# A two-layer decoder trunk: the first loads in smaller pieces, six warm-up matmuls instead of nine, and the last output tile in three column pieces

## The chip, the cores and the metric

The kernel runs on one core of one Trainium2 chip. The metric is the device time of a whole execution, in microseconds (us); lower is better. A core has five engines with an instruction stream each: TensorE (PE; its loads of the stationary operand are listed as PEld), VectorE (DVE), ScalarE (ACT), GpSimd (POOL) and SyncE (SP), which here only issues transfers (DMAs). They wait for each other by semaphores. The compiler of the kernel lays out the order of the instructions on each engine, and that order is kept when the program runs.

## What is computed

The reference is a trunk of two layers over 512 tokens with 16 learned "meta" tokens in front, 528 in all, with a width of 1024, in 32-bit floats. Cut to what matters:

```python
for l in range(DEPTH):                      # 2 layers
    h = rmsnorm(h_res, norm_gain[l])
    proj = h @ w_in[l]                      # 1024 -> 4640 columns
    u_pool, z_pool, c_q, c_kv, k_rope, z_mla, g_pool, g_mla = split(proj)
    y_pool = (pool_mix(u_pool, ...) * silu(z_pool)) @ pool_w_up[l]
    o_mla  = mla(c_q, c_kv, k_rope, pos, ...)           # 8 heads, causal attention
    y_mla  = (o_mla * silu(z_mla)) @ mla_w_up[l]
    merged = sigmoid(g_pool) * y_pool + sigmoid(g_mla) * y_mla
    h_res  = h_res + merged @ w_out[l]      # 1024 -> 1024
return h_res[:, N_META:]                    # the 512 tokens
```

## The kernel before

Activations are kept transposed: 128 features on the partitions, tokens along the columns. A width of 1024 is thus eight "depth" pieces of 128. To keep the precision of 32-bit numbers on PE, each operand is split into a high part (a rounded copy, made by ACT) and a low part (what the rounding left, made by DVE), and each product is three matmuls: high x high, high x low, low x high. This is `mm3` (lines 203 to 207): line 204 multiplies the high weights with the high tokens, 205 the high weights with the low tokens, 206 the low weights with the high tokens. Each of them loads its own 128x128 stationary tile of weights.

All large products go through one list, `plan`. Each entry (`Gemm`) is one tile of 128 output features; `stream()` (line 213) walks the list. It fetches the weights in chunks of up to 512 columns (four depth pieces, 256 KB), four chunks ahead, splits them in `wload` (lines 191 to 201), and multiplies. The tokens of a tile are cut into `segs`, column pieces with a PSUM buffer each: for every chunk of weights all pieces are walked, and within a piece four depth pieces, three matmuls each. When the last depth piece of a column piece is done, its evacuation `evac` runs. In layer 0 the pieces are two of 264 tokens (`FULL`, line 126), in layer 1 one of 512 (`XTOK`), since the meta tokens are dropped. The attention of eight heads, the statistics for the norms and the splits run beside this stream.

The start is written by hand, lines 141 to 173. The first chunk of weights (the first half of tile `ckv0`) is fetched into the buffer `rinv` by ACT's queue; SP issues the gains `gn` (24 KB), the first token tile `xb[:, 0]` (264 KB), the first chunk of `ckv1` into `raw`, and the second token tile. The other six token tiles, two more chunks and two tables are issued by `other_loads` (line 164); each waits until the transfer named `first` has landed, which is that of the gains:

```python
act.dma_start(early[0][:, 0:512], win[0, MT_CKV, :, 0:512])
first = sp.dma_start(gn, gains)
sp.dma_start(xb[:, 0, :T], xT[:, 0, :])
```

Line 157 then gives PE nine matmuls of 128 columns on a tile of ones, whose result nobody reads. A token tile is scaled with its gain and split by `split_h` (line 362): line 366 on ACT writes the high part `hh`, line 368 on DVE the low part `hl`; for the first tile this is done in two halves of 264 tokens, for the others at once. The split of the weights is line 199 (ACT) and 200 (DVE); the results of the first two chunks are in buffers named `th`, later ones in `whi` and `wlo`. The products of `ckv0` go to PSUM buffers named `S`, those of `ckv1` to `mm`.

The end is the product with `w_out` in layer 1, tiles `o0` to `o7`. Their evacuation is `ev_o`: SP fetches the residual rows from the scratch `scr` into a buffer `tmp` (line 1055; there are three such buffers), DVE adds them to half the product (line 1061), SP writes the output `yT` (line 1065). `o7` is the last work of the program, and the only tile of layer 1 that is cut into two column pieces, of 256 tokens each.

Of the kernel before, what the change touches and what calls it, by code (L numbers as in the profile page):

```python
# [9 lines left out]
F32 = mybir.dt.float32  # L10
# [3 lines left out]
AF = mybir.ActivationFunctionType  # L14
# [4 lines left out]
P = 128  # L19
DEPTH = 2  # L20
D = 1024
SEQ = 512
NM = 16
T = SEQ + NM
HALF = T // 2
# [10 lines left out]
MT_CKV = 0  # L36
# [21 lines left out]
BACK = 7800.0  # L58
LATE = 13000.0
RET = 12500.0  # L60
WARM = 9
NB = 10


# [16 lines left out]
def trunk(ctx, tc, xT, xrow, mrow, pos, win, wkr, wqb, wkb, wvb, wgr, wpu, wmu, wout, gains, const, yT):  # L81
    nc = tc.nc
    pe, act, dve, gp, sp = nc.tensor, nc.scalar, nc.vector, nc.gpsimd, nc.sync
# [11 lines left out]
    def nm(s):  # L95
        uid[0] += 1
        return f"{s}_{uid[0]}"

    def slot(tag, dt=F32, bufs=1, w=W):
        return sl.tile([P, w], dt, tag=tag, name=nm(tag), bufs=bufs)  # L100
# [7 lines left out]
    def wide():  # L108
        return tp.tile([P, NB * P], F32R, tag="th", name=nm("th"), bufs=2)
# [20 lines left out]
    gn = cp.tile([P, DEPTH * N_GAIN], F32, name="gn")  # L130
    xb = cp.tile([P, 8, W], F32, name="xb")
    early = []

    def fetch(src, n, raw, eng):
        eng.dma_start(raw[:, :n], src)
        return raw

    def rawt():
        return wp.tile([P, 512], F32, tag="raw", name=nm("raw"), bufs=3)

    early.append(slot("rinv"))
    act.dma_start(early[0][:, 0:512], win[0, MT_CKV, :, 0:512])
    first = sp.dma_start(gn, gains)
    sp.dma_start(xb[:, 0, :T], xT[:, 0, :])
    early.append(fetch(win[0, MT_CKV + 1, :, 0:512], 512, rawt(), sp))
    sp.dma_start(xb[:, 1, :T], xT[:, 1, :])
    xt = [xb[:, k] for k in range(8)]
# [7 lines left out]
    wps = pp.tile([P, 512], F32, tag="o", name="wps", bufs=1)  # L155
    for i in range(WARM):
        pe.matmul(wps[:, 0:P], ones, ones, start=True, stop=True)  # L157
# [31 lines left out]
    loads = [0]  # L189

    def wload(src, n, spare):
        raw = early.pop(0) if early else fetch(src, n, rawt(), sp)
        loads[0] += 1
        if loads[0] <= 2 or spare:
            t = wide()
            hi, lo = t[:, 0:512], t[:, 512:1024]
        else:
            hi, lo = (wp.tile([P, 512], F32R, tag=t, name=nm(t), bufs=3) for t in ("whi", "wlo"))
        act.activation(hi[:, :n], raw[:, :n], AF.Copy)  # L199
        dve.tensor_sub(lo[:, :n], raw[:, :n], hi[:, :n].bitcast(F32))  # L200
        return hi, lo

    def mm3(out, wh, wl, xh, xl, start, stop):
# [9 lines left out]
    def stream():  # L213
# [5 lines left out]
        def load(i):  # L219
            g_, c = flat[i]  # L220
            n = min(512, g_.width - c)
            return wload(g_.src[:, c:c + n], n, g_.spare)
# [120 lines left out]
    class Layer:  # L343
# [728 lines left out]
        def register(self, nxt):  # L1072
            l, XS = self.l, self.XS
            wi = lambda t: win[l, t]
            hs, ys, cs = (lambda: self.hs), (lambda: self.ys), (lambda: self.cs)

            def add(name, src, width, **kw):
                plan.append(Gemm((l, name), src, width, **kw))

            for m in range(2):  # L1080
                if (l, m) == (0, 1):
                    plan[-1].alloc = sct
                add(f"ckv{m}", wi(MT_CKV + m), D, evac=self.ev_ckv(m), xs=hs, segs=FULL)
            def cq(m):
                add(f"cq{m}", wi(MT_CQ + m), D, evac=self.ev_cq(m), xs=hs, segs=XS)

            def kk(p):
                add(f"k{p}", wkb[l, p], 256, evac=self.ev_k(p), xs=cs, segs=FULL)

            for m in range(5):  # L1090
                cq(m)
            for m in range(4):
                add(f"u{m}", wi(MT_U + m), D, evac=self.ev_u(m), xs=hs, segs=FULL)
                kk(m)
            def zp(m):
                add(f"zp{m}", wi(MT_ZP + m), D, evac=self.ev_silu(self.zps, "xa", m), xs=hs, segs=XS)

            def y(m):
                add(f"y{m}", wgr[l, m], P, evac=self.ev_y(m), xs=lambda: [self.ys[m]], segs=XS)

            add("v", wvb[l], 1024, body=self.v_body)
            zp(0)
            zp(1)
            y(0)
            zp(2)
            y(1)
            zp(3)
            y(2)
            cq(5)
            y(3)  # L1110
            for r in range(2):
                add(f"qr{r}", wqb[l, r], 768, evac=self.ev_qr(r), xs=lambda: self.cqs, segs=XS)
            for p in range(4):
                add(f"qn{p}", wqb[l, 2 + p], 768, evac=self.ev_qn(p), xs=lambda: self.cqs, segs=XS)
            for m in range(8):
                add(f"pu{m}", wpu[l, m], 512, evac=self.ev_pu(m), xs=ys, segs=XS)
            for m in range(4):
                add(f"zm{m}", wi(MT_ZM + m), D, evac=self.ev_silu(self.zms, "u", m), xs=hs, segs=XS)
            for m in range(8):
                add(f"gp{m}", wi(MT_GP + m), D, evac=self.ev_gp(m), xs=hs, segs=XS)  # L1120
            for m in range(8):
                add(f"gm{m}", wi(MT_GM + m), D, evac=self.ev_gm(m), xs=hs, segs=XS)
            for m in range(8):
                add(f"mu{m}", wmu[l, m], 512, evac=self.ev_mu(m), xs=lambda: self.ogs, segs=XS)
                plan[-1].spare = m % 2 == 1
                if (l, m) in ((0, 2), (0, 5)):
                    plan[-1].alloc = sct
            mg = lambda: self.mg
            for m in range(8):
                add(f"o{m}", wout[l, m], D, evac=self.ev_o(m, nxt), xs=mg,  # L1130
                    segs=[(NM, NM + SEQ // 2), (NM + SEQ // 2, T)] if self.last and m == 7 else XS)
                if (l, m) == (0, 1):
                    plan[-1].alloc = sct

# [151 lines left out]
```

## Time and profile before

| what | us |
|---|---|
| median of 3 runs | 758.31 |
| lowest and highest | 758.05, 759.73 |
| the profiled execution, whole | 758.87 |
| its span, first to last instruction | 756.0 |
| PE busy | 750.0 (99%) |
| DVE busy | 549.7 (73%) |
| ACT busy | 395.8 (52%) |

The profile is of one execution; its times are counted from the start of the span. A row of the timeline gives the start and the duration in us, the engine, the line of the kernel, the operation, what is written and read, shapes (partitions x elements), a count if several equal instructions were merged, and in brackets how long the engine had been idle and what ended it. Matmuls are pipelined: the duration of one is longer than the distance to the next, so their pace is read from the starts. SPq and ACTq are the engines' queues on which transfers are issued; the duration there is that of the issue, and the data land later. In a row of groups, after the count stand the busy time in us and the mean of one in ns. PEclk is the clock that was granted to PE, in tenths.

### The profile page before, as it was taken

The page shows a single profiled execution, that of the slowest core. Times are in us where ns is not written, and L with a number is a line of the kernel's source. Part 1 is how long each engine was busy: PE and PEld are TensorE (multiplying, and loading weights), DVE is VectorE, ACT ScalarE, POOL GpSimd, SP SyncE. Part 2 cuts the span into 40 slices and gives each one's busy share as a digit, 9 for nine tenths or more (in the row PEclk, how much of TensorE's full clock was granted, in tenths as well). Part 3 has the DMA queues.
Part 4 walks back from the last instruction along what each step waited for, and adds up shares of the span by engine and source line. Part 5 has one row for each costly group of instructions (what it writes and reads, how often), then busy time and mean ns, then how long its engine had stood idle before and what let it go on. Part 6 is the DMA issues. An engine that isn't in the chain of part 4 may idle for free.

```text
span 756.0 us, 14327 instructions
## 1 busy us (share of the span) xinstructions
PE 750.0 (99%) x5030; PEld 683.9 (90%) x5030; DVE 549.7 (73%) x1211; ACT 395.8 (52%) x864; POOL 219.0 (29%) x267
## 2 busy tenths in 40 slices
PE   9999999999999999999999999999999999999998
PEld 9999999999999999999997898887788888878887
DVE  5587787358999978784376487774578999966942
ACT  6755656545566656443364355455445656653321
POOL 2026305104463520160220263032054535101400
PEclk9999999999999999999999999999999999999999
DMA  8533223343756558425643333234438666773472
GB/s 287 173 101 101 85 86 87 119 120 120 212 166 192 167 152 216 116 86 166 182 124 98 102 94 90 82 90 125 127 110 230 171 159 202 191 178 89 130 229 83
DMA packets 72852, 106.57 MB, mean 141 GB/s; under 512 B 14102, under 2 KB 34966, under 8 KB 72780
## 3 DMA queue, kind: packets, MB, share of 16 engines
q1 hardware_dynamic: 72636, 105.39, 48.1%
q8 instruction: 39, 0.64, 0.4%
q14 instruction: 33, 0.27, 0.1%
q10 hardware_dynamic: 144, 0.26, 0.1%
HBM read 89.76 MB, written 15.86 MB: 140 GB/s over the span
## 4 chain that ended last, share of the span: by engine, by line
PE 95%; DMA 2%; DVE 2%; issue 0%; SPq 0%; ACT 0%; ACTq 0%
PE mm L206 28%; PE mm L204 28%; PE mm L205 28%; PE S L204 2%; PE S L205 2%; PE S L206 2%; DMA attE<-pdr 1%; PE o L972 1%; PE o L975 1%; PE S L530 1%; PE S L873 1%; DVE attE L951 1%; PE wps L157 1%; DMA pdr<-attD 1%; PE S L496 0%
## 5 line engine op out<-in xcount | busy, mean ns | idle before, releaser
L205 PE MATMUL mm<-hl,whi 128*128 128x264 f32 (+2 forms) x1072 | 336.5, 315 | 0.0
L206 PE MATMUL mm<-hh,wlo 128*128 128x264 f32 (+2 forms) x1072 | 336.0, 316 | 0.0
L204 PE MATMUL mm<-hh,whi 128*128 128x264 f32 (+2 forms) x1072 | 335.7, 315 | 0.0
L200 DVE TENSOR_TENSOR wlo<-raw,whi 128x512 fp32r<-128x512 f32 (+2 forms) x242 | 178.8, 742 | 93.4 <-ACT whi L199 90.3
L199 ACT ACTIVATE whi<-raw 128x512 fp32r<-128x512 f32 (+2 forms) x242 | 144.7, 601 | 180.0 <-PE mm L205 137.8
L204 PEld LDWEIGHTS mm<-hh,whi 128*128 128x128 f32 x1072 | 201.3, 188 | 13.6 <-ACT racc L640 0.4
L205 PEld LDWEIGHTS mm<-hl,whi 128*128 128x128 f32 x1072 | 201.6, 188 | 13.0
L206 PEld LDWEIGHTS mm<-hh,wlo 128*128 128x128 f32 x1072 | 200.8, 188 | 12.2
L644 POOL TENSOR_TENSOR racc<-racc,tmp 128x264 f32<-128x264 f32 (+1 forms) x15 | 14.3, 957 | 133.6 <-ACT tmp L643 133.6
L1047 POOL TENSOR_TENSOR tmp<-tmp,xb 128x264 f32<-128x264 f32 (+1 forms) x24 | 27.3, 1154 | 46.2 <-DVE tmp L1045 44.3
L803 POOL CAST qhl<-q 32x528 fp32r<-32x528 f32 (+1 forms) x32 | 27.9, 886 | 42.3 <-PE S L873 41.1
L825 DVE CUSTOM_DVE_ANT_0 S<-S,maskw,nqs 128x240 f32<-128x240 f32 (+4 forms) x80 | 37.8, 492 | 2.9 <-PE S L206 2.6
L801 POOL CAST kh<-cq 32x528 fp32r<-32x528 f32 x16 | 15.7, 980 | 71.0 <-issue 37.2
L204 PE MATMUL mm<-cq,whi 128*128 128x264 f32 (+1 forms) x108 | 34.8, 322 | 0.0
L205 PE MATMUL mm<-th,whi 128*128 128x264 f32 (+1 forms) x108 | 34.6, 321 | 0.0
L204 PE MATMUL mm<-u,whi 128*128 128x264 f32 (+1 forms) x108 | 34.6, 320 | 0.0
L206 PE MATMUL mm<-cq,wlo 128*128 128x264 f32 (+1 forms) x108 | 34.5, 321 | 0.0
L205 PE MATMUL mm<-cq,whi 128*128 128x264 f32 (+1 forms) x108 | 34.5, 321 | 0.0
L206 PE MATMUL mm<-u,wlo 128*128 128x264 f32 (+1 forms) x108 | 34.5, 319 | 0.0
L951 DVE TENSOR_TENSOR attE<-attE,th 128x640 fp32r<-128x640 f32 x32 | 28.1, 901 | 7.1 <-ACT th L950 7.1
L835 POOL COPY pm<-cq 128x16 f32<-128x16 f32 x32 | 19.2, 600 | 41.7 <-ACT cq L832 41.5
L832 ACT ACTIVATE cq<-S,bia 128x400 f32<-128x400 f32 (+2 forms) x48 | 24.4, 511 | 10.7 <-DVE bia L886 9.3
(302 smaller groups left out, 1362.8 us busy)
## 6 DMA issues: line engine op xcount, KB each, us to landing
raw<-win SPq DMA_DIRECT2D x143, 256.0 KB, 3.1
pdr<-attD SPq DMA_DIRECT2D x16, 640.0 KB, 4.3
attE<-pdr SPq DMA_DIRECT2D x64, 160.0 KB, 4.2
raw<-wout SPq DMA_DIRECT2D x32, 256.0 KB, 2.9
raw<-wpu SPq DMA_DIRECT2D x16, 256.0 KB, 2.7
raw<-wmu SPq DMA_DIRECT2D x16, 256.0 KB, 2.7
raw<-wqb SPq DMA_DIRECT2D x12, 256.0 KB, 2.6
xb<-xT SPq DMA_DIRECT2D x8, 264.0 KB, 5.5
```

What stands on the lines that cost most here:

```text
L199: act.activation(hi[:, :n], raw[:, :n], AF.Copy)
L200: dve.tensor_sub(lo[:, :n], raw[:, :n], hi[:, :n].bitcast(F32))
L204: first = pe.matmul(out, wh, xh, start=start, stop=False)
L205: pe.matmul(out, wh, xl, start=False, stop=False)
L206: newest[0] = pe.matmul(out, wl, xh, start=False, stop=stop)
L801: gp.tensor_copy(d[r0:r0 + 32, :], f[g0:g0 + 32, :])
L803: gp.tensor_copy(d[r0:r0 + 32, x0:T], f[g0:g0 + 32, x0:T])
L825: return dve.tensor_tensor_reduce(out=sv, in0=sv, in1=mask, scale=nqs[:, i, h:h + 1], scalar=3e38, op0=ALU.add, op1=ALU.min, accum_out=bia ...
L832: act.activation(pv, sv, AF.Exp, scale=-1.0, bias=bia[:, i:i + 1], accum_out=rs[:, c:c + 1])
L835: gp.tensor_copy(pm[:, i, 16 * odd:16 * odd + 16], pt[i][:, 0:NM])
L951: dve.tensor_sub(got[:, a:b], f[:, a:b], hi[:, a:b].bitcast(F32))
L1047: gp.tensor_add(t[:, :b - a], t[:, :b - a], self.am[m][:, a:b])
```

## The change

Three places are changed. At the start, the first chunk of weights comes as 128 columns on ACT's queue and 384 columns on SP's; the first token tile comes as two halves of 264 tokens; the gains go second on ACT's queue; and `first`, for which the later loads wait, is now the first half token tile. The split of the first chunk is done in the same two pieces, so that the first depth piece has a part of its own. PE gets six warm-up matmuls instead of nine. At the end, the tile `o7` is cut into column pieces of 256, 128 and 128 tokens instead of 256 and 256.

```diff
-WARM = 9
+WARM = 6
...
-    act.dma_start(early[0][:, 0:512], win[0, MT_CKV, :, 0:512])
-    first = sp.dma_start(gn, gains)
-    sp.dma_start(xb[:, 0, :T], xT[:, 0, :])
+    act.dma_start(early[0][:, 0:P], win[0, MT_CKV, :, 0:P])
+    first = sp.dma_start(xb[:, 0, :HALF], xT[:, 0, :HALF])
+    act.dma_start(gn, gains)
+    sp.dma_start(xb[:, 0, HALF:T], xT[:, 0, HALF:T])
+    sp.dma_start(early[0][:, P:512], win[0, MT_CKV, :, P:512])
     early.append(fetch(win[0, MT_CKV + 1, :, 0:512], 512, rawt(), sp))
     sp.dma_start(xb[:, 1, :T], xT[:, 1, :])
...
-        act.activation(hi[:, :n], raw[:, :n], AF.Copy)
-        dve.tensor_sub(lo[:, :n], raw[:, :n], hi[:, :n].bitcast(F32))
+        for a, b in ((0, P), (P, n)) if loads[0] == 1 else ((0, n),):
+            act.activation(hi[:, a:b], raw[:, a:b], AF.Copy)
+            dve.tensor_sub(lo[:, a:b], raw[:, a:b], hi[:, a:b].bitcast(F32))
...
                 add(f"o{m}", wout[l, m], D, evac=self.ev_o(m, nxt), xs=mg,
-                    segs=[(NM, NM + SEQ // 2), (NM + SEQ // 2, T)] if self.last and m == 7 else XS)
+                    segs=[(NM, NM + SEQ // 2), (NM + SEQ // 2, T - P), (T - P, T)] if self.last and m == 7 else XS)
```

## The prediction

> **What bounds the kernel now.** I read the page first (shares, then the chain that ended last), then the timeline of the first 10 us and of the last 10 us, and last the weight loads of the narrowest matmuls.
>
> ```profile
> span 756.0 us, 14327 instructions
> PE 750.0 (99%) x5030; PEld 683.9 (90%) x5030; DVE 549.7 (73%) x1211; ACT 395.8 (52%) x864; POOL 219.0 (29%) x267
> PEclk9999999999999999999999999999999999999999
> PE 95%; DMA 2%; DVE 2%; issue 0%; SPq 0%; ACT 0%; ACTq 0%
> ```
>
> TensorE (PE) is busy for 99% of the span and makes 95% of the chain. Nothing in the middle of the program is touched: the two compiled orders, line by line, differ only in the first dozen instructions of each engine and in the last tile. So the result is the sum of a start and an end, and each is worth a microsecond or two at most. The profiled execution took 758.87 us around its span of 756.0; the median of the runs is 758.31, so I work out differences on the profile and add them to the median. The three runs lie 1.68 us apart, which is 0.2% of the time; that is about what this measurement can tell from no change.
>
> The start, from the timeline of the first 10 us (start, duration, engine, line):
>
> ```profile
> 0.73 0.40 ACTq L142 DMA_DIRECT2D rinv<-win  x1
> 0.74 0.39 SPq L143 DMA_DIRECT2D gn<-gains  x1
> 1.19 0.41 SPq L144 DMA_DIRECT2D xb<-xT  x1
> 2.11 0.43 SPq L146 DMA_DIRECT2D xb<-xT  x1
> 2.46 0.20 ACT L150 ACTIVATE warm<-warm 128x1 f32<-128x1 f32 x1
> 3.37 0.80 SPq L166 DMA_DIRECT2D xb<-xT  x2
> 3.67 0.63 ACT L199 ACTIVATE th<-rinv 128x512 fp32r<-128x512 f32 x1 [1.01 <-DMA rinv<-win]
> 4.51 0.92 ACT L366 ACTIVATE hh<-xb,gn 128x264 fp32r<-128x264 f32 x2 [0.21 <-DMA xb<-xT]
> 5.34 0.62 ACT L199 ACTIVATE th<-raw 128x512 fp32r<-128x512 f32 x1
> 5.87 0.42 PE L205 MATMUL S<-hl,th 128*128 128x264 f32 x1
> 6.09 0.33 PE L206 MATMUL S<-hh,th 128*128 128x264 f32 x1
> 6.25 0.28 PE L204 MATMUL mm<-hh,th 128*128 128x264 f32 x1
> 6.38 0.28 PE L205 MATMUL mm<-hl,th 128*128 128x264 f32 x1
> 6.70 1.45 DVE L368 SCALAR_TENSOR_TENSOR hl<-xb,gn,hh 128x528 fp32r<-128x528 f32 x2
> 7.71 0.28 PE L205 MATMUL S<-hl,th 128*128 128x264 f32 x1
> 8.44 0.74 ACT L366 ACTIVATE hh<-xb,gn 128x528 fp32r<-128x528 f32 x1 [1.10 <-DMA xb<-xT]
> ```
>
> I see three things. The first real matmul waits for the token tile (ACT was idle for it until 4.51), not for the nine warm-up matmuls. Matmuls of 264 columns are 0.22 us apart at 5.87 and 6.09, and 0.13 apart from 6.25 on: PE runs slowly for its first five microseconds, although the granted clock of the page reads 9 throughout. And from 6.25 on PE never pauses, but its data come barely in time.
>
> **The start, step by step.**
>
> ```profile
> SPq L166 <- DMA gn<-gains: 0.8, 1, 0.8
> DMA to landing us min/median/max: 3.8/3.8/3.8
> L366 ACT ACTIVATE hh<-xb,gn 128x264 fp32r<-128x264 f32 x2 | 0.9, 509 | 0.2 <-DMA xb<-xT 0.2
> L199 ACT ACTIVATE whi<-raw 128x128 fp32r<-128x128 f32 x8 | 2.4, 305 | 4.2 <-PE mm L205 2.8 <-issue 1.4
> L157 PE MATMUL wps<-ones x18: 421/421/580, 1.1 to 4.8; 128*128 128x128 f32 x18
> 9.43 0.28 PE L204 MATMUL S<-hh,th 128*128 128x264 f32 x1
> ```
>
> Above: what SP waited for; the landing of the second token tile (L146); two casts of ACT; the warm-up matmuls (shortest, median, longest in ns, first and last start); the first use of the fourth token tile. The gains move from SP to second place on ACT's queue. Issued at 0.74 they landed when SP stopped waiting for them, at 3.37: 2.6 us. Issued at 1.13, behind one issue of 0.40, I expect them at 3.75 (from 3.4, if the smaller transfers ahead are quicker, to 4.1). ACT's own start is delayed by that issue from 2.66 to 3.06, which its idle 1.01 us covers; without that cover it costs 0.40. The 128-column piece of the weights is cast in 0.305, so by 3.6; then the first half of the tokens at 3.75, done at 4.26 by the row of 509 ns. First matmul at about 4.35, 0.7 before today's (5.08).
>
> SP issues two transfers more (0.46 each, from 0.74 and 1.19), so the second weight tile and the second token tile are issued 0.46 later. They landed 3.4 and 3.8 us after their issue, behind a full DMA, and the bytes ahead of them hardly differ, so I put their landing where it is (the second token tile at 2.11 + 3.8 = 5.9) and take 0.46 later as the other end. The later token tiles wait for the first half tile instead of the gains; that lands around 3.4, and they are issued from 3.37 as before.
>
> ACT then does both token halves (0.92, to 4.67), the other 384 columns of the weights (0.52, between the 0.305 of 128 and the 0.63 of 512), the second weight tile (0.62): 5.81, against 5.96 now. The split of one cast in two costs 0.2 there, and about as much on VectorE (DVE), hidden since both start 0.7 earlier. PE has all six matmuls of the first token tile done by then, where it has four done at 6.25 now.
>
> What is late next: the low half of the second token tile (DVE, 6.70 to 7.42) lets PE go on at 7.71 now; it depends on the landing at 5.9, which stays. PE can start there 0.24 earlier, not 0.7. Then the fourth token tile: its landing releases ACT at 8.44, the cast ends at 9.18, and PE uses it at 9.43; that slack of 0.25 is all a PE running ahead can take. **Start: 0.2 us less**; ends: 0.75 less (all of the first matmul's lead, if the later landings come forward too), and 0.25 more (transfers 0.46 later, the slack used up).
>
> Warm-up: 18 passes in 3.7 us from 1.1 to 4.8, so 0.218 each; twelve end by about 3.9, and PE is idle until 4.35, with short holes till 4.9. I cost this at nothing, as PE is still busy for three quarters of the time that precedes 6.1; what it costs if not is the first rival.
>
> **The end.** The last output tile takes three matmuls for each of eight depth pieces, 24 for each column piece: now two pieces (48 matmuls of 256 columns), then three (24 of 256, 48 of 128). The columns are the same; each matmul, however, loads its own 128x128 stationary tile, so 24 loads are added. The timelines of the end, and of the narrowest matmuls with full loads (144 columns, in the attention of the last head):
>
> ```profile
> 747.04 0.28 PE L204 MATMUL mm<-hh,whi 128*128 128x256 f32 x1
> 752.60 0.28 PE L206 MATMUL mm<-hh,wlo 128*128 128x256 f32 x1
> 747.24 0.69 DVE L1061 SCALAR_TENSOR_TENSOR tmp<-mm,tmp 128x512 f32<-128x512 f32 x1 [1.65 <-PE mm L206]
> 752.92 0.42 DVE L1061 SCALAR_TENSOR_TENSOR tmp<-mm,tmp 128x256 f32<-128x256 f32 x1 [0.99 <-PE mm L206]
> 655.41 0.19 PEld L873 LDWEIGHTS S<-kl,qhl 128*128 128x128 f32 x1
> 655.51 0.19 PEld L873 LDWEIGHTS S<-kh,qhl 128*128 128x128 f32 x1
> 655.63 0.19 PEld L204 LDWEIGHTS mm<-hh,whi 128*128 128x128 f32 x1
> 655.74 0.19 PEld L205 LDWEIGHTS mm<-hl,whi 128*128 128x128 f32 x1
> 654.04 0.22 PE L972 MATMUL o<-th,vt 128*128 128x128 f32 x1
> 654.10 0.23 PE L975 MATMUL o<-attE,vt 128*64 128x128 f32 x1
> 742.88 0.39 PE L204 MATMUL mm<-hh,whi 128*128 128x512 f32 x1
> 743.11 0.39 PE L205 MATMUL mm<-hl,whi 128*128 128x512 f32 x1
> yT<-tmp SPq DMA_DIRECT2D x5, 256.0 KB, 2.1
> yT<-tmp SPq DMA_DIRECT2D x2, 128.0 KB, 1.7
> ```
>
> 47 steps between 747.04 and 752.60 make 0.118 us per matmul of 256 columns; 512 take 0.23. Scaled by columns 144 would take 0.07 and 128 would take 0.06. But the loads around the 144-column matmuls start 0.11 apart (0.33 for three steps): the load sets the pace there, hidden at 256 columns and bare at 128. A pair with a load of only 64 columns does go 0.06 apart (654.04, 654.10), which fits. I take 0.11, the row nearest in shape: 48 x 0.11 = 5.28 instead of 24 x 0.118 = 2.83, **2.45 us more** on PE, all on the path. Ends: 0.06 each (loads hidden), 0.05 more; 0.14, the longest step in that group, 3.9 more.
>
> The Trainium skill, "TensorE: Matmul & The Clock Gate", section "LDWEIGHTS (loading the stationary operand)", gives a load as its columns at 1.2 GHz, 107 ns for 128; this trace agrees with its 0.11, and by the page's figure the added PE time would be an estimated 2.3. It is the rule that speaks against the third piece.
>
> What the smaller last piece gives back: its eviction by DVE is 0.42 for 256 and 0.69 for 512 columns, so about 0.29 for 128, 0.13 less; the output transfer lands in 2.1 us at 256 KB and 1.7 at 128 KB, so 1.5 at 64 KB, 0.2 less. One residual fetch and one output issue more lie on SP, idle there; the third piece's fetch waits for the buffer of the tile before, whose output is issued near 748 and lands by 750, five microseconds before the eviction that uses it (else each microsecond late counts in full). **End: 2.45 - 0.13 - 0.2 = 2.1 us more.**
>
> Sum: 2.1 - 0.2 = 1.9 us more: 760.8 on the profiled execution's 758.87, 760.2 on the median, 0.25% slower.
>
> **The rivals.**
>
> The clock comes late. PE speeds up near 6.2, 5.1 us after it began, with no hole before. With six warm-ups it has holes of about 0.8 us in the 3.4 us before that. If it then stays slow for that long again, to 9.6, matmuls go 0.22 apart: PE has done 12 by 7.2 and 11 more by 9.6, 23, where today it has done 31 by then; eight times 0.12 is 1.0 us more instead of 0.2 less. 758.31 + 2.1 + 1.0 = 761.4. Against it: the holes are short. The Trainium skill's same page, "The HAM clock gate", has the clock opened by a busy window of 3.4 us that runs freely; the granted clock in this trace does not show it, the spacing of the matmuls does.
>
> Not slower: the third piece's loads hide after all. 144-column matmuls come only three at a time here, between wide ones, and in a run of 48 the loads might be drawn ahead, as they are at 256 columns. At 0.06 each, 2.9 for 48, the end is 0.05 - 0.33 = 0.3 less, and with the start 0.5 less: 757.8. It decides against my forecast wherever a narrow matmul goes under about 0.1 us (a sum under 1.5). Against it: the loads after those three were still 0.11 apart. The section "Back-to-back issue gap" of that page has a stream of 128-column matmuls with their loads at 81 ns, an estimated 758.8; no run of equal matmuls of that width is in this trace.
>
> The start gives all: if the fourth token tile lands earlier by what the first does, 0.75 us come off: 758.31 + 2.1 - 0.75 = 759.7. For it: gains and half tiles are off the head of the queue. Against it: its landing follows the bytes before it, which stay.
>
> **How the numbers follow.** My forecast 0.62 (759.6 to 760.8), the late clock 0.15, hidden loads 0.10, the full start 0.13. Slower by over 0.2% is above 759.8: 0.58 of my forecast and the late clock, 0.73. Within 0.2%: the rest of my forecast, the full start, most of the hidden loads, 0.23. Faster: both last rivals at once, 0.04. The range, 759.0 to 761.6, holds the forecast, the full start and nearly all of the late clock.
>
> **What would show it.** In the profile after: first matmul near 4.3 to 4.4; matmul pace 0.12 from about 6.2; the use of the fourth token tile near 9.2; the 128-column matmuls of the last tile 0.11 apart, and the time from the first 256-column matmul of it to the last eviction 8.3 instead of 5.9; a last eviction of 0.29. I am wrong if narrow matmuls run at 0.06 to 0.08, or if PE stays at 0.22 past 7.

## The result, and the profile after

The changed kernel takes 763.3 us in the median (six runs, 761.95 to 764.54), the kernel before 758.18 beside it (six runs, 756.74 to 760.02): a ratio of 1.0069, with a 95% interval of 1.0055 to 1.0083, or 4.2 to 6.3 us more. Forecast were 1.9 us more. The direction was right, the size was not. The profiled execution took 764.46 us around its span of 762.6, so it is one of the longer ones; against the profiled execution before, its span is 6.6 longer, against 5.1 in the medians.

The page of the kernel after: span, engines, and the shares of the chain that ended last.

```profile
span 762.6 us, 14375 instructions
PE 754.4 (99%) x5048; PEld 687.8 (90%) x5048; DVE 549.8 (72%) x1213; ACT 396.0 (52%) x865; POOL 217.4 (29%) x267
PEclk9999999999999999999999999999999999999999
PE 97%; DMA 2%; DVE 1%; SPq 0%; issue 0%; ACT 0%
```

PE is as busy as before and still makes the chain, so the shares tell nothing of the loss. Three marks along the run show where it arises. They are the first matmul of the sums for a norm, the first 256-column matmul of the last tile, and the last eviction. The first row below is the first mark in the kernel before, whose other two stand in the prediction (747.04 and 752.92); the rows after it are of the kernel after. Columns are start, duration, engine, line.

```profile
26.34 0.65 PE L421 MATMUL mm<-q,ones 128*32 128x264 f32 x8
```

```profile
29.69 0.65 PE L424 MATMUL mm<-q,ones 128*32 128x264 f32 x8
751.37 0.28 PE L207 MATMUL mm<-hh,whi 128*128 128x256 f32 x1
757.05 0.27 PE L209 MATMUL mm<-hh,wlo 128*128 128x128 f32 x1
759.40 0.28 PE L209 MATMUL mm<-hh,wlo 128*128 128x128 f32 x1
759.71 0.29 DVE L1064 SCALAR_TENSOR_TENSOR tmp<-mm,tmp 128x128 f32<-128x128 f32 x1 [1.05 <-PE mm L209]
yT<-tmp SPq DMA_DIRECT2D x2, 64.0 KB, 1.5
```

By the first mark, 26.34 against 29.69, the kernel after is already 3.35 us behind in these two executions: that is the start. At the last tile it is 4.33 behind (747.04 against 751.37); a wait for the attention of the last head, of a kind that both executions have, was longer by 0.8 in this one (1.93 and 0.65 instead of 0.93 and 0.89), and nothing in the change touches it. From there to the end of the last eviction 8.63 us pass instead of 6.30 (747.04 to 753.34): the end costs 2.33. The 128-column matmuls go 0.112 apart (21 steps from 757.05 to 759.40), the last eviction takes 0.29, and the last output of 64 KB lands in 1.5 us.

So the end did what was forecast, and the start, forecast at 0.2 less, is the surprise. Its timeline after:

```profile
1.05 2.93 PE L159 MATMUL wps<-ones 128*128 128x128 f32 x12 [1.05 <-DVE na L759]
2.11 0.43 SPq L135 DMA_DIRECT2D raw<-win  x1
2.58 0.43 SPq L148 DMA_DIRECT2D xb<-xT  x1
3.49 0.31 ACT L202 ACTIVATE th<-rinv 128x128 fp32r<-128x128 f32 x1 [0.34 <-DMA rinv<-win]
3.98 0.92 ACT L369 ACTIVATE hh<-xb,gn 128x264 fp32r<-128x264 f32 x2 [0.18 <-DMA gn<-gains]
4.54 1.00 PE L207 MATMUL S<-hh,th 128*128 128x264 f32 x2 [0.56 <-ACT hh L369]
5.31 0.52 ACT L202 ACTIVATE th<-rinv 128x384 fp32r<-128x384 f32 x1 [0.41 <-DMA rinv<-win]
6.00 0.42 PE L209 MATMUL S<-hh,th 128*128 128x264 f32 x1
6.73 0.63 ACT L202 ACTIVATE th<-raw 128x512 fp32r<-128x512 f32 x1 [0.90 <-DMA raw<-win]
7.41 0.59 PE L207 MATMUL mm<-hh,th 128*128 128x264 f32 x1 [0.99 <-ACT th L202]
7.60 1.41 ACT L369 ACTIVATE hh<-xb,gn 128x528 fp32r<-128x528 f32 x2 [0.24 <-DMA xb<-xT]
12.42 0.42 PE L208 MATMUL S<-hl,th 128*128 128x264 f32 x1
12.64 0.33 PE L209 MATMUL S<-hh,th 128*128 128x264 f32 x1
12.81 0.28 PE L207 MATMUL S<-hh,th 128*128 128x264 f32 x1
12.93 0.28 PE L208 MATMUL S<-hl,th 128*128 128x264 f32 x1
```

The first real matmul does come earlier (4.54 instead of 5.08). But the first chunk of the second weight tile, `raw`, is cast at 6.73, ACT having waited 0.90 for its landing; before it was cast at 5.34 without a wait. It lands 4.6 us after its issue at 2.11, where it took 3.4 after 1.65. PE runs out of work and idles 0.99 us before 7.41. And matmuls of 264 columns stay 0.22 apart up to 12.42, where before they went 0.13 apart from 6.25 on. The transfers show why the chunk is late. Windows of half a microsecond, the last two numbers of a row are the mean busy share of the core's DMA engines and GB/s; first the kernel before, then after:

```profile
3.00:3.50 0.50, 0.50 (x4) 0.50 (x4) 0.00 (x0) 0.00 (x0) 0.46 (x2) 1.00 1.02 394
4.00:4.50 0.50, 0.50 (x4) 0.50 (x4) 0.17 (x1) 0.30 (x1) 0.32 (x4) 1.00 1.06 411
5.00:5.50 0.50, 0.50 (x4) 0.30 (x2) 0.47 (x3) 0.50 (x3) 0.00 (x0) 1.00 1.01 389
```

```profile
3.00:3.50 0.50, 0.50 (x4) 0.50 (x4) 0.00 (x0) 0.16 (x2) 0.46 (x2) 1.00 1.16 204
4.00:4.50 0.50, 0.00 (x0) 0.00 (x0) 0.13 (x1) 0.50 (x2) 0.32 (x4) 1.00 0.72 230
5.00:5.50 0.50, 0.50 (x3) 0.50 (x3) 0.43 (x2) 0.19 (x1) 0.00 (x0) 1.00 0.80 240
```

Before, the transfers run at about 400 GB/s up to 5.5; after, they fall to about half of that from 3.0 on, though the bytes of these first loads are the same in sum.

### The profile page after: what moved, and what is told of

Its sections match the earlier page's. It is cut to its first block, busy times and chain, and to the rows that moved or that the text cites. A ratio compares the mean times of both kernels' runs of the same rounds, so it can differ in the third digit from the quotient of the medians.

```text
span 762.6 us, 14375 instructions
## 1 busy us (share of the span) xinstructions
PE 754.4 (99%) x5048; PEld 687.8 (90%) x5048; DVE 549.8 (72%) x1213; ACT 396.0 (52%) x865; POOL 217.4 (29%) x267
## 4 chain that ended last, share of the span: by engine, by line
PE 97%; DMA 2%; DVE 1%; SPq 0%; issue 0%; ACT 0%
PE mm L207 29%; PE mm L209 29%; PE mm L208 28%; PE S L207 2%; PE S L208 2%; PE S L209 2%; PE o L975 1%; PE o L978 1%; DMA attE<-pdr 1%; PE S L533 1%; PE S L876 1%; DMA raw<-win 1%; PE S L499 0%; DVE attE L954 0%; DMA racc<-mdr 0%; PE mm L990 0%
## 5 line engine op out<-in xcount | busy, mean ns | idle before, releaser
L806 POOL CAST qhl<-q 32x528 fp32r<-32x528 f32 (+1 forms) x32 | 25.3, 804 | 46.9 <-PE S L876 45.6
L953 ACT ACTIVATE th<-attE 128x640 fp32r<-128x640 f32 x32 | 21.8, 728 | 16.5 <-DMA racc<-mdr 6.6
```

Of the source, the lines that this page charges most:

```text
L806: gp.tensor_copy(d[r0:r0 + 32, x0:T], f[g0:g0 + 32, x0:T])
L953: behind(act.activation(hi[:, a:b], f[:, a:b], AF.Copy), newest[0])
```

## The experiments

The changes are shown against the kernel before unless said otherwise. Each ratio is to runs of the kernel before on the same chip. "First mark" is the start of the first matmul of the sums for a norm (26.34 before, 29.69 after). Kernels with an idle transfer compute all that the kernel before does.

### The change in two halves

The end alone:

```diff
-  segs=[(NM, NM + SEQ // 2), (NM + SEQ // 2, T)] if self.last and m == 7 else XS)
+  segs=[(NM, NM + SEQ // 2), (NM + SEQ // 2, T - P), (T - P, T)] if self.last and m == 7 else XS)
```

> The kernel before, with only the last tile cut into three column pieces (256, 128, 128). If the narrow matmuls wait for their 128-column loads (0.11 us each), the end is 2.1 to 2.3 us longer and the rest stays: ratio about 1.0028 to the kernel before. If the whole added time of the changed kernel came from its start, the ratio is 1.000.

Measured: 760.54 against 758.4, 1.0025 (1.0012 to 1.0038), 0.9 to 2.9 us more. The first mark is at 26.28, as before. The last tile of this kernel:

```profile
746.51 0.28 PE L204 MATMUL mm<-hh,whi 128*128 128x256 f32 x1
754.54 0.28 PE L206 MATMUL mm<-hh,wlo 128*128 128x128 f32 x1
754.85 0.29 DVE L1061 SCALAR_TENSOR_TENSOR tmp<-mm,tmp 128x128 f32<-128x128 f32 x1 [1.05 <-PE mm L206]
```

From the first matmul of the tile to the end of its last eviction it takes 8.63 us, as in the kernel after. The end is worth what was forecast.

The start alone, with six warm-up matmuls and then with nine (the difference of the two is only this number):

```diff
-WARM = 9
+WARM = 6
...
-    act.dma_start(early[0][:, 0:512], win[0, MT_CKV, :, 0:512])
-    first = sp.dma_start(gn, gains)
-    sp.dma_start(xb[:, 0, :T], xT[:, 0, :])
+    act.dma_start(early[0][:, 0:P], win[0, MT_CKV, :, 0:P])
+    first = sp.dma_start(xb[:, 0, :HALF], xT[:, 0, :HALF])
+    act.dma_start(gn, gains)
+    sp.dma_start(xb[:, 0, HALF:T], xT[:, 0, HALF:T])
+    sp.dma_start(early[0][:, P:512], win[0, MT_CKV, :, P:512])
```

> The changed kernel with the last tile in two column pieces again: only the start is changed (pieces, gains on ACT's queue, six warm-ups). If start and end add up, 2.9 to 3.0 us longer than before (ratio about 1.004); the second weight tile lands near 6.7 and PE is at the slow pace of 0.22 us until long after 7. By my prediction's step it would be 0.2 us shorter.

> The start in pieces, but nine warm-up matmuls, and the last tile in two pieces. Theory A (the missing warm-ups keep PE slow): the pace turns to 0.12 near 6 to 7, only the late second weight tile is left, 0.9 us longer than before (1.001). Theory B (the late second weight tile opens a hole of 1 us near 6.5 and that keeps PE slow): the pace turns as late as with six, 2.5 to 3 us longer (1.0035 to 1.004).

Measured: with six 761.0, 1.0031 (1.0021 to 1.0042), 1.6 to 3.2 us more; with nine 759.87, 1.0016 (1.0005 to 1.0026). End and start together make 1.9 + 2.4 = 4.3 by their ratios, within the interval of the whole change (4.2 to 6.3). The chunk `raw` is cast at 6.85 and 6.53, and the first mark lies at 28.77 and 28.07. With nine, PE is fast from 5.15 and still waits 1.26 for the chunk:

```profile
5.15 0.29 PE L208 MATMUL S<-hl,th 128*128 128x264 f32 x1
7.21 0.39 PE L207 MATMUL mm<-hh,th 128*128 128x264 f32 x1 [1.26 <-ACT th L202]
```

So there are two losses at the start: the late chunk, which is there with a fast PE too (1.2 us by the ratio with nine), and the slow PE, about as much again with six by the medians, though the intervals of the two ratios overlap.

Six warm-up matmuls alone:

```diff
-WARM = 9
+WARM = 6
```

> The kernel before with six warm-up matmuls instead of nine, nothing else. Theory A: PE has a hole from 3.9 to 5.1 and stays at 0.22 us to 9 or later, 1 to 2.5 us longer (1.0015 to 1.003). Theory B: the loads land as before, the pace turns near 6.2 as before, no change (1.000).

Measured: 758.56, 0.9996 (0.9984 to 1.0007), no difference. In the profiled execution, the longest of its thirteen (762.43), PE was slow until 8.9 and the first mark at 27.54, 1.2 late. The loads were as early as before (`raw` cast at 5.40). Fewer warm-ups cost something in some executions, and by the median nothing as long as the data come in time.

The opposite, the start of the change with thirteen, so that PE is busy without a hole until the data come:

```diff
-WARM = 9
+WARM = 13
```

(on top of the start with nine)

> The start in pieces, the last tile in two pieces, but 13 warm-up matmuls, so that PE is busy nearly until the second weight chunk lands near 6.7 to 7.2. Theory A (holes keep or make PE slow): the pace is 0.12 by 7.5, and 1.0 to 1.4 us are left of the 2.4 that six warm-ups cost, from the late loads alone (1.0013 to 1.0018). If PE's pace had no part in it, the 2.4 stay (1.003).

Measured: 759.83, 1.0023 (1.0011 to 1.0035), no better than nine, and between the two values expected, so it decides nothing on PE's pace. PE is fast by 7.2 and has no hole before it, the first mark is at 28.35. The late loads are not mended by it: `raw` is cast at 6.37 and the second token tile is only there at 8.02.

### Which of the new transfers delays the chunk

The token tile in halves, and nothing else; then the weights in two pieces, the second on SP's queue, and nothing else. In this kernel and the later ones with the weights in pieces, the first chunk is also cast in these two pieces, as in the change:

```diff
-    sp.dma_start(xb[:, 0, :T], xT[:, 0, :])
+    sp.dma_start(xb[:, 0, :HALF], xT[:, 0, :HALF])
+    sp.dma_start(xb[:, 0, HALF:T], xT[:, 0, HALF:T])
```

> The kernel before with the first token tile in two halves, nothing else (nine warm-ups, gains first, weights whole on ACT's queue). Theory Q (three quarters of the first weight chunk were moved from ACT's queue to SP's, and one queue alone does not keep the transfers going): nothing moves, the cast of the second weight chunk starts near 5.4, the rate stays near 400 GB/s until 5.5, ratio 1.000. Theory P (more and smaller transfers are slow as such): that cast starts 0.4 to 0.8 later, the rate falls earlier, ratio 1.0005 to 1.001.

```diff
-    act.dma_start(early[0][:, 0:512], win[0, MT_CKV, :, 0:512])
+    act.dma_start(early[0][:, 0:P], win[0, MT_CKV, :, 0:P])
     first = sp.dma_start(gn, gains)
     sp.dma_start(xb[:, 0, :T], xT[:, 0, :])
+    sp.dma_start(early[0][:, P:512], win[0, MT_CKV, :, P:512])
```

> The kernel before with the first weight chunk in two pieces, 128 columns on ACT's queue and 384 on SP's, nothing else. Theory Q: most of the loss is here: the rate falls to 170 to 280 GB/s from 3 us on, the cast of the second weight chunk starts at 6.3 or later, 1 to 1.5 us longer (1.0013 to 1.002). Theory P: half of it, that cast near 5.8, 0.5 us longer.

Measured: halves 759.4, 1.0020 (1.0002 to 1.0038); weights 760.66, 1.0029 (1.0019 to 1.004). The casts of the chunk, first with the halves, then with the weights in pieces:

```profile
6.51 0.63 ACT L200 ACTIVATE th<-raw 128x512 fp32r<-128x512 f32 x1 [1.31 <-DMA raw<-win]
```

```profile
7.53 0.63 ACT L201 ACTIVATE th<-raw 128x512 fp32r<-128x512 f32 x1 [2.15 <-DMA raw<-win]
```

Each of the two makes the chunk late by itself, and each puts one transfer more ahead of it on SP's queue. The bytes issued ahead of the chunk are the same in the first, and moved from one queue to the other in the second. That the change put more of the early bytes on SP's queue, so that ACT's queue lost its share, is not needed: the halves move nothing.

All of the weights on ACT's queue, with the rest of the changed start (`raw` is then third on SP's, as before the change); and only the gains moved to ACT's queue:

```diff
-    sp.dma_start(early[0][:, P:512], win[0, MT_CKV, :, P:512])
+    act.dma_start(early[0][:, P:512], win[0, MT_CKV, :, P:512])
```

(on top of the start with nine)

> The start in pieces with nine warm-ups and the last tile in two pieces, but the 384 columns of the first weight chunk are on ACT's queue too, behind the gains. Theory Q: the two queues share the load as before the change, the rate stays near 400, the second weight chunk lands near 5.1, and the start is 0 to 0.5 us shorter than before (1.000 to 0.9993). Theory P: as with the 384 columns on SP's queue, 1.2 us longer (1.0016).

```diff
-    first = sp.dma_start(gn, gains)
-    sp.dma_start(xb[:, 0, :T], xT[:, 0, :])
+    first = sp.dma_start(xb[:, 0, :T], xT[:, 0, :])
+    act.dma_start(gn, gains)
```

> The kernel before with only the gains moved to second place on ACT's queue; the first token tile is first on SP's and releases the later loads. The planner then puts other instructions in another order, so only the transfers are read. Theory Q: the rate stays near 400 GB/s to 5.5 and the second weight chunk lands by 5.0. If the gains on ACT's queue (128 packets of 192 bytes) are the cause, the rate falls to 170 to 280 from 3 us as in the changed kernel.

Measured: weights on ACT's queue 760.1, 1.0022 (1.0006 to 1.0037), with `raw` cast at 7.21 after a wait of 2.31. So the place on SP's queue alone does not set the landing. Gains moved: a single execution of 759.28, in which the compiled order differs too, with `raw` cast at 5.41 but the first weights only at 4.80 (3.67 before); the gains are the only small transfer, and the rate stays near 400 GB/s from 3.0 to 5.0. One execution settles nothing on the time, since those of one kernel lie several microseconds apart.

### What a transfer ahead costs

An idle transfer, whose data nobody reads, is put on SP's queue just ahead of the chunk: first the gains once more (24 KB, 128 rows), then their first 16 rows (3 KB):

```diff
     sp.dma_start(xb[:, 0, :T], xT[:, 0, :])
+    sp.dma_start(idle, gains)
```

> The kernel before with one more transfer on SP's queue, just ahead of the second weight chunk: the gains once more (24 KB, 128 rows of 192 bytes) into a buffer that nothing reads. Theory R (each transfer of 128 rows costs the loads about 1 us, whatever its size): the cast of the second weight chunk starts 1 us or more later than 5.4, PE waits there, 1 to 2 us longer (1.0013 to 1.0026). Theory S (only bytes count): 24 KB are 0.06 us at 400 GB/s, no change (1.000).

```diff
     sp.dma_start(xb[:, 0, :T], xT[:, 0, :])
+    sp.dma_start(idle[0:16, :], gains[0:16, :])
```

> As the one before, but the idle transfer has 16 rows (3 KB). If a transfer costs by itself, the second weight chunk is as late as with 128 rows; if its rows cost (theory R in its narrow form, about 1 us for 128), it is 0.1 us late and the time does not change (1.000).

The same 24 KB behind the first weights on ACT's queue, and just behind the chunk on SP's:

```diff
     act.dma_start(early[0][:, 0:512], win[0, MT_CKV, :, 0:512])
+    act.dma_start(idle, gains)
```

> The idle transfer of 128 rows is on ACT's queue instead, behind the first weight chunk. If both queues share what makes a transfer slow, the second weight chunk is late by 1 us or more as with the one on SP's queue (1.0013 to 1.0026); if each queue has its own, it lands as before and only ACT's start is 0.4 us later, which is hidden (1.000).

```diff
     early.append(fetch(win[0, MT_CKV + 1, :, 0:512], 512, rawt(), sp))
+    sp.dma_start(idle, gains)
```

> The kernel before with the idle transfer of 24 KB just behind the second weight chunk on SP's queue instead of ahead of it. If the place on the queue decides: the second weight chunk lands as before (its cast starts at 5.3 to 5.5), the second token tile, now fifth, is 1 us late (its cast near 7), and less is lost than with the idle transfer ahead: 0 to 1 us. If any additional transfer slows all loads from the start, the chunk is late too (6.5).

Measured: ahead of the chunk, 24 KB 758.92, 1.0015 (1.0002 to 1.0028), and 3 KB 758.94, 1.0016 (1.0006 to 1.0025); on ACT's queue 757.72, 0.9991 (0.9978 to 1.0004); behind the chunk 757.63, 0.9996 (0.9983 to 1.0008). The cast of the chunk in these four, in this order:

```profile
6.56 0.63 ACT L201 ACTIVATE th<-raw 128x512 fp32r<-128x512 f32 x1 [1.11 <-DMA raw<-win]
```

```profile
6.45 0.63 ACT L201 ACTIVATE th<-raw 128x512 fp32r<-128x512 f32 x1 [1.01 <-DMA raw<-win]
```

```profile
5.48 0.61 ACT L201 ACTIVATE th<-raw 128x512 fp32r<-128x512 f32 x1
```

```profile
5.32 0.62 ACT L201 ACTIVATE th<-raw 128x512 fp32r<-128x512 f32 x1
```

When the chunk is issued and lands, in us, and when the first of its 128 packets starts and the last ends (packets of 2,048 bytes on SP's queue; one execution of each kernel):

| kernel | issued | first packet starts | last packet ends | lands |
|---|---|---|---|---|
| before | 1.65 | 3.68 | 4.65 | 5.07 |
| 24 KB ahead on SP's queue | 2.12 | 3.87 | 6.18 | 6.53 |
| 3 KB ahead on SP's queue | 2.12 | 3.76 | 6.13 | 6.42 |
| 24 KB on ACT's queue | 1.65 | 3.66 | 4.79 | 5.24 |
| 24 KB behind it | 1.65 | 3.67 | 4.71 | 5.11 |
| tokens in halves | 2.12 | 3.33 | 6.14 | 6.49 |
| weights in two pieces | 2.11 | 3.83 | 7.16 | 7.50 |
| after | 2.11 | 3.69 | 6.35 | 6.71 |
| changed start, all weights on ACT's queue | 1.65 | 2.91 | 6.77 | 7.18 |

One transfer more ahead of the chunk on its own queue makes it land 1.4 us later, 0.47 by the later issue and 0.9 to 1.0 on the way, and ACT waits 1.0 to 1.1 for it, whether that transfer has 3 KB or 24, 16 rows or 128. At 400 GB/s 3 KB are under 0.01 us and 24 KB 0.06: neither bytes nor rows are what is paid for. On the other queue it costs 0.2 that ACT does not feel, and behind the chunk nothing. No run delays the issue alone, so it is not ruled out that a later issue costs more than its own 0.47.

The packets show where the time goes. The chunk is begun hardly later, if at all: its first packet starts at most 0.2 after that of the kernel before. In the kernels with a late chunk the packets are spread over 2.3 us or more instead of 1.0. At least half of the 128 still take 84 ns each, as all of them do before, but between 6 and 23 take over 200. The rate falls with it: from 4.0 to 4.5 in the kernel with 24 KB ahead, and in that with 24 KB behind:

```profile
4.00:4.50 0.50, 0.50 (x4) 0.50 (x4) 0.09 (x1) 0.37 (x1) 0.32 (x4) 1.00 0.51 151
```

```profile
4.00:4.50 0.50, 0.50 (x4) 0.50 (x4) 0.12 (x1) 0.35 (x2) 0.32 (x4) 1.00 1.07 385
```

In the first the DMA engines have nothing to move for half of that time (busy share 0.51), although the chunk was long issued. In the kernel after, the share was 1.16, 0.72 and 0.80 in the three windows shown, so idle engines are not the whole of its low rate.

Two more arrangements that keep the count on SP's queue as it was: both pieces of the weights on ACT's queue, and the halves of the tokens with the gains moved to ACT's:

```diff
-    act.dma_start(early[0][:, 0:512], win[0, MT_CKV, :, 0:512])
+    act.dma_start(early[0][:, 0:P], win[0, MT_CKV, :, 0:P])
+    act.dma_start(early[0][:, P:512], win[0, MT_CKV, :, P:512])
```

> The kernel before with the first weight chunk in 128 and 384 columns, both on ACT's queue; SP's queue is as before. If the place on SP's queue decides: the second weight chunk's cast starts at 5.3 to 5.6, no change or up to 0.3 us shorter (1.000 to 0.9996). If smaller pieces on ACT's queue slow SP's transfers: 6.5 or later, 1 to 2 us longer.

```diff
-    first = sp.dma_start(gn, gains)
-    sp.dma_start(xb[:, 0, :T], xT[:, 0, :])
+    first = sp.dma_start(xb[:, 0, :HALF], xT[:, 0, :HALF])
+    act.dma_start(gn, gains)
+    sp.dma_start(xb[:, 0, HALF:T], xT[:, 0, HALF:T])
```

> The kernel before with the first token tile in two halves first on SP's queue and the gains second on ACT's queue, weights whole. The second weight chunk keeps third place on SP's queue. If the place decides: its cast starts at 5.1 to 5.6, 0 to 0.4 us shorter (1.000 to 0.9995). If half tiles are slow as such: 6.5, 1 to 1.5 us longer (1.0015 to 1.002).

Measured: weights 758.81, 1.0014 (0.9999 to 1.0029); tokens 758.73, 1.0013 (0.9997 to 1.0029). Neither is better than the kernel before, and whether they are worse is not settled. Both casts of the chunk lie between the two times expected. With the weights in pieces the first of them is cast early, at 3.06, but the token tile is late:

```profile
5.02 0.92 ACT L368 ACTIVATE hh<-xb,gn 128x264 fp32r<-128x264 f32 x2 [1.66 <-DMA xb<-xT]
6.26 0.62 ACT L201 ACTIVATE th<-raw 128x512 fp32r<-128x512 f32 x1
```

With the tokens in halves the rate holds at 380 to 393 GB/s from 3.0 to 5.0 and the chunk is cast at 5.84, right behind the tokens; it is the first weights that come late, at 4.35 instead of 3.67. In each arrangement something that PE needs first came later by half a microsecond or more (tokens 5.02 instead of 4.51, weights 4.35 instead of 3.67).

Why the packets are spread is not shown. A cost per transfer, whatever its size, by which small transfers use up a lead that large ones keep (one of 256 KB takes 0.65 us at 400 GB/s), would fit the idle engines (the 0.51 above). That the chunk as a whole is made ready a microsecond later does not fit, since its first packet is not. Nor does a strict order per queue: it gives no reason for the late chunk with all of the weights on ACT's queue (cast at 7.21), nor for the second token tile, which comes in time behind the idle transfer (cast at 6.02, where near 7 was expected). How two queues share such a cost stays open too.

### When PE is slow

The profile of the kernel with the tokens in halves shows the clock itself. Windows of one microsecond: length, busy time of PE, PEld, DVE, ACT and POOL, and last the granted clock, the DMA share and GB/s.

```profile
6.00:7.00 1.00, 0.09 (x1) 0.00 (x0) 0.00 (x0) 0.49 (x1) 0.00 (x0) 1.00 0.92 332
7.00:8.00 1.00, 0.81 (x4) 0.81 (x5) 0.78 (x2) 0.88 (x2) 0.00 (x0) 0.68 1.07 296
8.00:9.00 1.00, 1.00 (x7) 1.00 (x7) 0.68 (x1) 0.47 (x1) 0.00 (x0) 0.50 0.96 353
10.00:11.00 1.00, 1.00 (x7) 1.00 (x6) 1.00 (x3) 0.92 (x2) 0.00 (x0) 0.61 1.04 400
```

PE was fast at 5.80, idled 1.11 us before 7.19, and then ran at half its clock: 0.68 puts the change at 7.36, 0.61 the return at 10.78, 3.42 us later. The kernel with the weights in two pieces shows the same after its wait of 2.16 (0.50 from 8.5 to 11.9). So a late chunk is paid for twice in some executions: by the wait, and by the clock after it, 3.4 us at half the pace, about 1.7 us. In the kernel after, the clock reads 1.00 all the same while matmuls go 0.22 apart up to 12.7, as it does up to 6.2 in the kernel before: the first slow stretch of these two executions does not show in this reading. That it lasted without a break in the kernel after is read from the matmuls, of which none between 4.54 and 12.4 is fast; the wait from 6.4 to 7.41 has none.

## Why the prediction was wrong

**The end: right.** 0.112 us per 128-column matmul, as taken from the loads around the 144-column ones; an eviction of 0.29 and an output of 1.5, as scaled. Forecast were 2.1, the two traces show 2.33 up to the last eviction and the end alone costs 0.9 to 2.9. The rival of hidden loads falls: there is no narrow matmul under 0.1 in 21 steps. Only the first step of each run of narrow ones, right behind the 256-column matmuls, takes 0.06 to 0.07 (752.78 to 752.85, 756.88 to 756.94); a load is hidden there, and not in the run. The Trainium skill's figure for the load ("TensorE: Matmul & The Clock Gate", section "LDWEIGHTS (loading the stationary operand)"), 107 ns for 128 columns, agrees with the 112 of the trace; the 81 ns of its section "Back-to-back issue gap" do not hold for this stream, which takes 112.

**The start: wrong, by 2.6 us.** The step that failed is that of the second weight tile: "the bytes ahead of them hardly differ, so I put their landing where it is ... and take 0.46 later as the other end". It landed 1.4 to 2.4 us later in every kernel of the table with a further transfer ahead of it on its queue (1.64 in the kernel after), against an end of 0.46; with all of the weights on ACT's queue it landed 2.1 later though its issue and its place on SP's queue were as before. I counted bytes and the issue, and the landing follows neither. The idle transfers show it without the rest of the change. (The prediction counts two transfers more on SP's queue; with the gains moved away it is one, as its 0.46 has it.) What I had as fixed was the time in which the chunk's packets pass: 1.0 us before and 2.7 after, from the same start. The times ahead of that step came nearly right and did not matter: the gains landed at 3.9 (forecast 3.75, range up to 4.1), the first matmul came at 4.54 (4.35). What I named as late next, the low half of the second token tile and the fourth token tile, was preceded by the chunk, which I had put last on ACT's chain at 5.81; that cast ended at 7.36.

**The warm-ups, costed at nothing: wrong here, and open alone.** The holes with six, 0.56 and 0.99 us, go with a PE that stayed slow until 12.7; with the start alone it was until 10.4. The rival of the late clock had the mechanism and was too small: it let the clock come at 9.6, at 1.0 us more, and had no late chunk. By the two starts with nine and six warm-ups the slow PE costs 1.1 us in the medians; with six in the kernel before it costs nothing that can be measured. The number of warm-ups thus mattered only together with the late chunk: the two edits are not a sum of two costs. By this pair, of the start's 2.4 us about 1.2 are the late chunk and 1.1 the slow PE; the split is loose, since with thirteen warm-ups and a fast PE 1.7 (1.0023) were still lost. The Trainium skill ("TensorE: Matmul & The Clock Gate", section "The HAM clock gate") has the clock opened by a window of 3.4 us that runs freely; stepping back from 12.75 by 3.41 a time gives 9.34 and 5.93 as an estimate of earlier ends of windows, and the one between holds the wait of 0.99. That agrees, and it isn't shown, as the trace doesn't record the windows.

**Full gain of the start: fell**, for the same reason. Its condition was that the fourth token tile lands earlier; ACT was released by a landed token tile at 9.18, where it was at 8.44 before.

**The sum.** 1.9 for the end and 2.4 for the start, each by its own runs, are 4.3 of the 5.1 measured. The rest is within the intervals; whether the two halves cost more together isn't settled.

## What to carry to other kernels

Count the transfers ahead of the one that the chain waits for next, not only their bytes: cutting the first load lets the first matmul start earlier, but a further transfer ahead of it on the queue pushed the next load back by 1.4 us here, at 3 KB as at 24. Moving pieces to the other queue did not cure it here. Cut into column pieces of fewer than 256 only where fewer loads of weights come with it: a matmul that loads its own 128-column tile cost 0.11 us at 128 columns and 0.118 at 256. And a wait of PE near its start has to be priced with what its clock does afterwards, not by its length alone.

## What the runs showed of the hardware that was not expected

A transfer of 3 KB in 16 rows delays the one behind it as much as one of 24 KB in 128 rows (landing at 6.4 and 6.5 instead of 5.1), and one of 24 KB on ACT's queue hardly does (5.2), in one execution of each. What grows is not the time to the chunk's first packet but the time in which its packets pass. The Trainium skill, "DMA: Bandwidth & Descriptors", section "Issuing engines are not separate DMA queues", says that using several engines to start transfers saves only the time of the issue; here the chunk's issue differs by 0.47 and its landing by 1.3 (6.53 against 5.24), so the trace does not agree.

PE loses its clock after waits much shorter than the slow stretch that follows. With six warm-ups in the kernel before, far from the start, it waited 1.78 and 0.52 us for the attention of the last head; windows of that execution, with the granted clock third from the end:

```profile
680.00:681.00 1.00, 1.00 (x5) 0.76 (x5) 1.00 (x2) 0.97 (x3) 0.37 (x1) 1.00 0.01 4
681.00:682.00 1.00, 0.48 (x3) 0.17 (x2) 1.00 (x3) 1.00 (x3) 0.00 (x0) 0.60 0.00 0
687.00:688.00 1.00, 1.00 (x4) 0.71 (x4) 0.76 (x2) 0.95 (x3) 0.00 (x0) 0.50 0.10 39
688.00:689.00 1.00, 1.00 (x6) 0.81 (x5) 0.97 (x2) 0.44 (x1) 0.00 (x0) 0.99 0.06 14
```

From 681.2 to 688.0 the clock was 0.50: 6.8 us, twice 3.4, and half of it, 3.4 us, lost. That is nearly the distance of this execution from the median of its kernel (762.43 against 758.56), though its late first mark should count in it too. The kernel after waited as long at that place (1.93 and 0.65) and kept its clock. This goes some way to explain why executions of one kernel lie more than 5 us apart: of 116 executions of the kernel before, the 89 with a mean granted clock of 1.000 took 758.1 on average, the 16 with 0.998 took 760.1, and the two with 0.995 took 762.2; nine with 0.999 took 757.5, so the smallest dips make no difference that can be seen. Whether a given wait has this consequence could not be foretold from its length.
